# A decoder layer on one core: first key and value weights in four 512-column pieces, factors sent through memory, keys' root from a square root

## The chip, the cores and the metric

The kernel runs on one core of one Trainium2 chip. Times are device microseconds (us) of one launch. Engines are called as in the profile: PE (matrix products), PEld (its weight loads), DVE (vector), ACT (scalar, with tables of functions), POOL (general), SP (here only a queue that issues transfers, DMAs).

## What is computed

One layer of a decoder on 512 tokens of width 1024 in float32. The change touches only the start: the norm of the input, and the key and value columns of the input projection.

```python
def rms_norm(x, g):
    y = xf * lax.rsqrt(jnp.mean(xf * xf, axis=-1, keepdims=True) + EPS)
    return y * g
...
    u = rms_norm(x, norm_mix_g[l])
    proj = u @ w_in[l]
    q = proj[..., :Q_END]                  # 1024 columns, 16 heads of 64
    k = proj[..., Q_END:K_END]             # 256 columns, 4 heads
    v = proj[..., K_END:V_END]             # 256 columns
    glu_in = proj[..., V_END:GLU_END]      # 2048 columns
    gate_attn, gate_conv = jnp.split(proj[..., GLU_END:], 2, axis=-1)
    k = rms_norm(k, k_norm_g[l])
    attn = sliding_window_attention(q, k, v, attn_sinks[l], rel_bias) @ w_attn_o[l]
    conv = conformer_conv(glu_in, ...)
    x = x + (sigmoid(gate_attn) * attn + sigmoid(gate_conv) * conv) @ w_out[l]
    x = x + square(relu(rms_norm(x, norm_mlp_g[l]) @ w_ff1[l])) @ w_ff2[l]
```

## The kernel before

**Numbers in two parts.** Each float32 operand a of a product is split into a high part (a copy rounded to the PE's fast float32 format, made on ACT or DVE) and a low part (a minus the high part, made on DVE or POOL). A product a·b is then three products on PE: high·high, low·high and high·low.

**Input.** The 512 tokens are four tiles of 128. `uTh` and `uTl` hold the high and low part of the normalized input, transposed: 1024 channels in 8 blocks k of 128, by 512 tokens. Tiles 2 and 3 come transposed from memory (`xc`, line 239) and are multiplied by the gain (`act_gain`, `dve_gain`) and then by the token's factor 1/rms. Tiles 0 and 1 come as they are (`load_x`) and are transposed on PE (`x_trans`, line 279). To start early, their first products use the input with the gain alone; the factor, a number for each token, is put in afterwards, when the result leaves PSUM (the argument `scale` of `heads_raw` and `keep_value`). For all later products tiles 0 and 1 are multiplied by their factors too, and split again (`x_scale`, `x_hi`, `x_lo`). `x_scale` needs the factors of a tile in a row, the same row in each of the 128 partitions: `cols_spread` (line 314) makes it with a product on PE into PSUM, `rsb`.

**Keys and values.** The 256 key columns and 256 value columns of the weights come in two halves of 512 rows each (`load_kv`, line 217: four transfers of 512 KB, rows of 256 numbers). High parts lie in `gates`, low parts in `qTt`. For tile 0 the keys and the values are separate products of 256 columns (`first_proj`, line 330: 24 each); for tiles 1 to 3 one product of 512 columns does both (`kv_proj`, line 1376: 24 for each tile). Each tile's result leaves PSUM by three ACT operations and two DVE operations: the raw keys (line 259), their squares (261), the values' high part (345), the squares' sums by head (262) and the values' low part (346).

**Order.** Up to here the order of PE, DVE, ACT and POOL is written out by hand, in the last function (from line 1411): each engine works in the order in which its instructions stand there. The transfers on SP also go in order. After it come all other steps, sorted by positions in units of PE work: first `columns` (the bias table's row `rel`, and two halvings of convolution constants), then the gate and value tiles of the convolution (`ps_g`, `ps_a`: `T_tile`, line 494, 24 products of 512 columns each, which need `uTh` and `uTl` of all four tiles), with `k_norm` (line 390) behind the first of them. `k_norm` makes the 16 factors of the keys on DVE with the integer trick and three Newton steps (`rsqrt`, line 102: 11 small operations behind `mean_eps`), then multiplies the keys. The keys are split (`k_hi`, `k_lo`) and transposed on PE (`k_stage`, `ktp`).

**Warm-up.** `warm_up` (line 206) gives PE products of no use while the first transfers are under way.

Of the kernel before, what the change touches and what calls it, by code (L numbers as in the profile page):

```python
# [8 lines left out]
F32 = mybir.dt.float32  # L9
# [3 lines left out]
ALU = mybir.AluOpType  # L13
# [27 lines left out]
WARM = 6  # L41
FILL = 4
FILL2 = 4
# [11 lines left out]
def tile_hybrid_block(  # L55
# [38 lines left out]
    def bc(ap, n):  # L94
        return ap.partition_broadcast(n)
# [109 lines left out]

    def warm_up(n):
        for _ in range(n):
            pe.matmul(warm, ident, ident, start=True, stop=True)
# [18 lines left out]
    kw_raw = wp.tile([P, KD, 256], F32, name="raw_k", tag="raw", bufs=2)  # L227
    load_kv(kw_raw, Q_END, 0)
    load_kv(kw_raw, Q_END, 1)
    xt.append(load_x(1))  # L230
    vw_raw = wp.tile([P, KD, 256], F32, name="raw_v", tag="raw", bufs=2)
    load_kv(vw_raw, K_END, 0)
    load_kv(vw_raw, K_END, 1)
# [21 lines left out]
    kw, vw = ([w[:, i] for w in (gates, qTt)] for i in range(2))  # L255
# [61 lines left out]

    def x_scale(t, half):
        u = us[t, half] = ps1.tile([P, 4, P], F32, name=f"uc_{t}{half}", tag="tr")
        ve.tensor_tensor(out=u, in0=xc[t][:, both(half), :],  # L320
                         in1=rsb[t].unsqueeze(1).to_broadcast([P, 4, P]), op=ALU.mult)

    def w_hi(w, raw, j, copy):
        copy(w[0][:, 4 * j:4 * j + 4, :], raw[:, 4 * j:4 * j + 4, :])

    def w_lo(w, raw, j, eng):
        ks = slice(4 * j, 4 * j + 4)
        eng.tensor_tensor(out=w[1][:, ks, :], in0=raw[:, ks, :], in1=w[0][:, ks, :].bitcast(F32), op=ALU.subtract)

    def first_proj(w, name):  # L330

        ps = ps1.tile([P, 256], F32, name=f"ps_{name}_0", tag="mm")
        for j in range(2):
            for u in (uTh, uTl):
                for k in range(4 * j, 4 * j + 4):
                    pe.matmul(ps, u[:, k, 0:P], w[0][:, k, :], start=(k == 0 and u is uTh), stop=False)
            yield
        for j in range(2):
            for k in range(4 * j, 4 * j + 4):
                pe.matmul(ps, uTh[:, k, 0:P], w[1][:, k, :], start=False, stop=(k == KD - 1))  # L340
            yield ps
# [23 lines left out]

    def columns():
        rel_ps = ps1.tile([P, P], F32, name="rel_ps", tag="s")
        pe.matmul(rel_ps[0:NQ, :], rb, oh, start=True, stop=True)
        ve.memset(rel, NEG)
        ve.tensor_scalar(out=wcol[:, :, 0:CW], in0=wcol[:, :, 0:CW], scalar1=0.5, scalar2=None, op0=ALU.mult)  # L370
        ve.tensor_scalar(out=lnh, in0=wcol[:, :, CW + 1:CW + 3], scalar1=0.5, scalar2=None, op0=ALU.mult)
        ve.tensor_copy(rel[:, P:2 * P], rel_ps[0:NQ, :])
        nc.sync.dma_start(rel_d, rel)
# [15 lines left out]

    def k_norm():  # L390
        ve.scalar_tensor_tensor(out=gk, in0=gk, scalar=HD ** -0.5, in1=gq, op0=ALU.mult, op1=ALU.mult)
        ve.tensor_scalar(out=nsink, in0=nsink, scalar1=-1.0, scalar2=None, op0=ALU.mult)
        rk = rsqrt(mean_eps(ssk, HD, 16, "k"), 16, "k")
        ve.tensor_tensor(out=k3, in0=k3, in1=rep(rk, HD), op=ALU.mult)
        ve.tensor_tensor(out=k3, in0=k3, in1=gk.unsqueeze(1).to_broadcast([P, 16, HD]), op=ALU.mult)
# [980 lines left out]
    def kv_proj(t, scale=1.0):  # L1376

        ps = ps1.tile([P, S], F32, name=f"ps_kv_{t}", tag="mm")
        for j in range(2):
            for k in range(4 * j, 4 * j + 4):  # L1380
                pe.matmul(ps, uTh[:, k, t * P:(t + 1) * P], gates[:, :, k, :], start=(k == 0), stop=False)
            yield
        for j in range(2):
            for k in range(4 * j, 4 * j + 4):
                pe.matmul(ps, uTl[:, k, t * P:(t + 1) * P], gates[:, :, k, :], start=False, stop=False)
            yield
        for j in range(2):
            for k in range(4 * j, 4 * j + 4):
                pe.matmul(ps, uTh[:, k, t * P:(t + 1) * P], qTt[:, :, k, :], start=False, stop=(k == KD - 1))
            yield  # L1390
        ksum = heads_raw(ps[:, 0:256], kraw, ssk, t, scale)
        vlow = keep_value(t, ps[:, 256:S], scale)
        yield
        ksum()
        vlow()
        yield
# [14 lines left out]
    with tc.manual_schedule(engines=START_ENGINES):  # L1411
        se.activation(roots[:, 0:1], epsc, AF.Sqrt)
        x_square(0, ss0)
        x_trans(0)
        load(0)
# [4 lines left out]
        w_hi(kw, kw_raw, 0, ve.tensor_copy)  # L1420
        w_hi(kw, kw_raw, 1, se.copy)
        r0 = root_steps(root[0], ss0, 1, "x0")
        next(r0)
        for half in range(2):
            x_lo(0, half)
            next(r0)
        w_lo(kw, kw_raw, 0, ve)
        next(r0)
        w_lo(kw, kw_raw, 1, ve)
        kp = first_proj(kw, "k")  # L1430
        next(kp)
        next(kp)
        x_trans(1)
        x_square(1, ss1)
        next(kp)
        ps = next(kp)
        w_hi(vw, vw_raw, 0, se.copy)
        w_hi(vw, vw_raw, 1, se.copy)
        ksum = heads_raw(ps, kraw, ssk, 0, root[0])
# [3 lines left out]
        vp = first_proj(vw, "v")  # L1443
        next(vp)
        next(vp)
        w_lo(vw, vw_raw, 0, ve)
# [35 lines left out]
        vlow()  # L1482
        next(kv)
        for half in range(2):
            x_lo(2, half)
        next(kv)
        kv = kv_proj(2)
        next(kv)
        next(kv)
# [5 lines left out]
        for _ in range(3):  # L1495
            next(kv)
        cols_spread(0, root[0])
# [5 lines left out]
        next(kv)  # L1503
        next(kv)
        next(kv)
        split_hi(0)
        split_lo(0)
        kv = kv_proj(3)
        next(kv)
        next(kv)  # L1510
        cols_spread(1, root[1])
# [5 lines left out]
        for _ in range(4):  # L1517
            next(kv)
        split_hi(1)
        split_lo(1)  # L1520
        split_hi(2)
        split_lo(2)
        next(kv)
        next(kv)
# [47 lines left out]
```

## Time and profile before

| what | value |
|---|---|
| time, median of 3 runs | 753.98 us (753.32 to 754.54) |
| the profiled execution's own time | 753.16 us |
| its span, first to last instruction | 751.4 us |
| PE busy | 744.0 us (99%) |
| DVE, ACT, POOL busy | 616.5, 445.4, 270.8 us |
| first product of the first gate tile `ps_g` | at 33.42 us |
| last product ends | by 747.9 us |

The span is what the profile shows of one execution; 1.76 us of that execution's time lie outside it. A row of the timeline has the start and the length of an instruction or of some merged ones (us), the engine, the line, the operation, the tiles (out<-in), the shapes, and in brackets the idle time ahead of it with what ended it. Merged instructions on an engine overlap a little, so the pace is read from start to start.

### The profile page before, as it was taken

The page shows a single profiled execution, that of the slowest core. Times are in us where ns is not written, and L with a number is a line of the kernel's source. Part 1 is how long each engine was busy: PE and PEld are TensorE (multiplying, and loading weights), DVE is VectorE, ACT ScalarE, POOL GpSimd, SP SyncE. Part 2 cuts the span into 40 slices and gives each one's busy share as a digit, 9 for nine tenths or more (in the row PEclk, how much of TensorE's full clock was granted, in tenths as well). Part 3 has the DMA queues.
Part 4 walks back from the last instruction along what each step waited for, and adds up shares of the span by engine and source line. Part 5 has one row for each costly group of instructions (what it writes and reads, how often), then busy time and mean ns, then how long its engine had stood idle before and what let it go on. Part 6 is the DMA issues. An engine that isn't in the chain of part 4 may idle for free.

```text
span 751.4 us, 11472 instructions
## 1 busy us (share of the span) xinstructions
PE 744.0 (99%) x4358; PEld 653.8 (87%) x4358; DVE 616.5 (82%) x942; ACT 445.4 (59%) x708; POOL 270.8 (36%) x213
## 2 busy tenths in 40 slices
PE   8999999999999999999999999999999999999997
PEld 7889988898888888888888899988998899889986
DVE  6879998888978988887437679899779977998795
ACT  7745467767666566248325457764676467546761
POOL 0364788948675565524450002210121012101210
PEclk9999999999999999999999999999999999999999
DMA  9341041214132122523228206983598359834772
GB/s 334 126 142 57 30 140 57 87 55 139 59 113 85 57 73 96 185 96 105 96 80 307 85 29 114 262 199 98 152 222 199 100 141 221 200 113 127 164 158 112
DMA packets 66071, 97.99 MB, mean 130 GB/s; under 512 B 3248, under 2 KB 36576, under 8 KB 66016
## 3 DMA queue, kind: packets, MB, share of 16 engines
q1 hardware_dynamic: 56768, 79.44, 31.7%
q0 software_dynamic: 9248, 17.83, 13.5%
q8 instruction: 34, 0.56, 0.3%
q14 instruction: 21, 0.17, 0.1%
HBM read 95.13 MB, written 2.12 MB: 129 GB/s over the span
## 4 chain that ended last, share of the span: by engine, by line
PE 98%; DMA 1%; SPq 0%; ACT 0%; DVE 0%; issue 0%; DVEq 0%
PE ps_x L1186 12%; PE ps_z L1191 12%; PE ps_y L1191 6%; PE ps_y L1186 6%; PE ps_z L1186 3%; PE ps_x L1191 3%; PE ps_g L503 2%; PE ps_q L192 2%; PE ps_q L194 2%; PE ps_q L193 2%; PE ps_a L503 2%; PE ps_ta L503 2%; PE ps_a L505 2%; PE ps_g L505 2%; PE ps_ta L505 2%; PE ps_g L504 2%
## 5 line engine op out<-in xcount | busy, mean ns | idle before, releaser
L1157 DVE TENSOR_TENSOR piecel<-block,pieceh 128x1024 fp32r<-128x1024 f32 x112 | 135.9, 1222 | 28.1 <-ACT pieceh L1154 27.8
L1154 ACT CAST pieceh<-block 128x1024 fp32r<-128x1024 f32 x112 | 116.7, 1050 | 69.6 <-DVE block L1147 23.4
L812 DVE SCALAR_TENSOR_TENSOR cv<-h,wcol,cv 128x512 f32<-128x512 f32 x208 | 146.1, 746 | 0.5
L1133 POOL DMA_DIRECT2D block<-in_w_ff_dram x34 | 41.3, 1246 | 287.3 <-DVE piecel L1157 150.3
L1186 PE MATMUL ps_x<-xSh,pieceh 128*128 128x256 f32 x192 | 53.0, 276 | 0.0
L1186 PE MATMUL ps_x<-xSl,pieceh 128*128 128x256 f32 x192 | 53.0, 276 | 0.0
L1186 PE MATMUL ps_x<-xSh,piecel 128*128 128x256 f32 x192 | 53.0, 276 | 0.0
L720 ACT ACTIVATE s<-s,negm 128x257 f32<-128x257 f32 (+1 forms) x64 | 30.4, 479 | 16.4 <-DVE negm L712 16.4
L1191 PE MATMUL ps_z<-piecel,aSh 128*128 128x512 f32 (+1 forms) x98 | 37.9, 387 | 0.0
L1191 PE MATMUL ps_z<-pieceh,aSh 128*128 128x512 f32 (+1 forms) x98 | 37.7, 385 | 0.0
L1191 PE MATMUL ps_z<-pieceh,aSl 128*128 128x512 f32 (+1 forms) x98 | 37.7, 385 | 0.0
L1147 DVE TENSOR_TENSOR block<-block,block 128x1024 f32<-128x1024 f32 x30 | 36.6, 1223 | 0.8 <-DMA block<-in_w_ff_dram 0.3
L804 POOL TENSOR_TENSOR side<-side,tap 128x512 f32<-128x512 f32 x24 | 31.1, 1296 | 15.1 <-ACT tap L803 15.1
L192 PE MATMUL ps_q<-wh_q,uTh 128*128 128x256 f32 x128 | 36.5, 286 | 0.0
L194 PE MATMUL ps_q<-wh_q,uTl 128*128 128x256 f32 x128 | 36.2, 283 | 0.0
L193 PE MATMUL ps_q<-wl_q,uTh 128*128 128x256 f32 x128 | 36.2, 283 | 0.0
L1186 PEld LDWEIGHTS ps_x<-xSh,pieceh 128*128 128x128 f32 x192 | 36.0, 188 | 0.0
L1186 PEld LDWEIGHTS ps_x<-xSl,pieceh 128*128 128x128 f32 x192 | 36.0, 188 | 0.0
L1186 PEld LDWEIGHTS ps_x<-xSh,piecel 128*128 128x128 f32 x192 | 36.0, 188 | 0.0
L744 DVE TENSOR_TENSOR pTl<-ptp,pTh 128x512 fp32r<-128x512 f32 x28 | 19.1, 687 | 17.2 <-ACT pTh L740 17.2
L729 POOL TENSOR_TENSOR s<-s,r 128x1024 f32<-128x1024 f32 (+1 forms) x16 | 26.9, 1684 | 17.0 <-DVE r L724 17.0
L471 POOL TENSOR_TENSOR wl_g<-raw_g,wh_g 128x1024 fp32r<-128x1024 f32 x8 | 19.5, 2432 | 31.8 <-ACT wh_g L467 31.8
(346 smaller groups left out, 2505.0 us busy)
## 6 DMA issues: line engine op xcount, KB each, us to landing
block<-in_w_ff_dram SPq DMA_DIRECT2D x64, 512.0 KB, 5.6
block<-in_w_ff_dram POOLq DMA_DIRECT2D x34, 512.0 KB, 6.9
x<-in_x_dram SPq DMA_DIRECT2D x8, 512.0 KB, 5.0
raw_g<-in_w_in_dram SPq DMA_DIRECT2D x8, 512.0 KB, 5.0
raw_q<-in_w_in_dram SPq DMA_DIRECT2D x8, 512.0 KB, 3.9
raw_a<-in_w_in_dram SPq DMA_DIRECT2D x8, 512.0 KB, 4.3
raw_ta<-in_w_in_dram SPq DMA_DIRECT2D x8, 512.0 KB, 3.9
raw_tc<-in_w_in_dram SPq DMA_DIRECT2D x8, 512.0 KB, 3.9
```

The lines of the kernel that those rows point to most:

```text
L192: pe.matmul(ps, ah, wh, start=first, stop=False)
L193: pe.matmul(ps, ah, wl, start=False, stop=False)
L194: pe.matmul(ps, al, wh, start=False, stop=last)
L503: pe.matmul(ps, wh[:, k, :], ah(k), start=(k == 0), stop=False)
L505: pe.matmul(ps, wl[:, k, :], ah(k), start=False, stop=(k == KD - 1))
L812: ve.scalar_tensor_tensor(out=cps[ct], in0=src, scalar=w, in1=cps[ct], op0=ALU.mult, op1=ALU.add)
L1133: ge.dma_start(tl["raw"][buf][:, ks, :], block(ph, i, j)[:, ks, :], accum_op=ALU.add)
L1147: ve.tensor_tensor(out=o, in0=a, in1=b, op=ALU.add)
L1154: se.copy(piece("h", n), tl["raw"][buf][:, 2 * h:2 * h + 2, :])
L1157: ve.tensor_tensor(out=piece("l", n), in0=tl["raw"][buf][:, 2 * h:2 * h + 2, :], in1=piece("h", n).bitcast(F32), op=ALU.subtract)
L1186: pe.matmul(o, b[:, c, w], a[:, k, :], start=(first and c + q + i == 0), stop=(k == 3 and i == 2), skip_group_check=True)
L1191: pe.matmul(acc[:, cols], a[:, k, w], b[:, c, cols], start=(first and c + i == 0), stop=(k == 3 and i == 2), skip_group_check=True)
```

## The change

1. The key and value weights come in four pieces of 256 rows by all 512 columns (`load_kv(i)`: 512 KB each, rows of 512 numbers), the first ahead of tile 1 of the input and the other three behind it. High and low parts are made by piece.
2. The products of tile 0 are now 24 of 512 columns. `kv_part` gives products by piece and kind ("h": high·high, "l": input's low part, "w": weights' low part), and those of tiles 0 and 1 are interleaved by hand so that they follow the pieces. Tile 1 is transposed ahead of the first product.
3. The factors of tiles 0 and 1 in a row no longer come from `cols_spread`. `spread_first` writes the two columns to memory and reads them back into every partition; `rows_up` copies that to PSUM on ACT.
4. The keys' factors start from a square root on ACT (`k_root`), a reciprocal and one Newton step (`rsqrt_root`): 4 small DVE operations behind `mean_eps` in place of 11.
5. On DVE the two halvings (`channel_halves`), the products of constants (`head_scales`) and the filling of `rel` stand earlier; `split_hi/lo` of the first three weight pieces of the later tiles stand earlier on ACT and POOL. The small loads of `vecs` and `bucket` stand ahead of the first `load`.
6. 8 instead of 6 warm-up products, on a constant 1.0 that is there before `ident`.

The code, cut to its core:

```diff
-WARM = 6
+WARM = 8
+    one = nc.const_aps.tensor(1.0, (P, P), F32)
-            pe.matmul(warm, ident, ident, start=True, stop=True)
+            pe.matmul(warm, one, one, start=True, stop=True)
-    def load_kv(raw, c0, kh):
-        nc.sync.dma_start(raw[:, 4 * kh:4 * kh + 4, :],
-                          w_in[512 * kh:512 * kh + 512, c0:c0 + 256].rearrange("(k p) c -> p k c", p=P))
+    def load_kv(i):
+        nc.sync.dma_start(kv_raw[i // 2][:, 2 * (i % 2):2 * (i % 2) + 2, :],
+                          w_in[256 * i:256 * i + 256, Q_END:Q_END + S].rearrange("(k p) c -> p k c", p=P))
...
+    def spread_first():
+        nc.sync.dma_start(first_d.rearrange("t p -> p t"), roots[:, 0:2])
+        nc.sync.dma_start(first_rows, bass.AP(tensor=first_d.tensor, offset=first_d.offset, ap=[[0, P], [P, 2], [1, P]]))
+    def rows_up():
+        rows = ps1.tile([P, 2, P], F32, name="rows", tag="s")
+        se.copy(rows, first_rows)
+        for t in range(2):
+            rsb[t] = rows[:, t, :]
...
+    def k_root():
+        k2["root"] = sm.tile([P, 16], F32, name="y_k", tag="y16")
+        se.activation(k2["root"], ssk, AF.Sqrt, scale=1.0 / HD, bias=epsc)
     def k_norm():
-        rk = rsqrt(mean_eps(ssk, HD, 16, "k"), 16, "k")
+        rk = rsqrt_root(k2["root"], mean_eps(ssk, HD, 16, "k"), 16, "k")
...
+    def kv_part(t, parts, kinds):
+        if t not in kvs:
+            kvs[t], done[t] = (ps1.tile([P, S], F32, name=f"ps_kv_{t}", tag="mm") if t else aux.tile([P, S], F32, name="ps_kv_0", tag="aux")), 0
+        for i in parts:
+            for kind in kinds:
+                for k in (2 * i, 2 * i + 1):
+                    u, w = {"h": (uTh, gates), "l": (uTl, gates), "w": (uTh, qTt)}[kind]
+                    done[t] += 1
+                    pe.matmul(kvs[t], u[:, k, t * P:(t + 1) * P], w[:, :, k, :], start=done[t] == 1, stop=done[t] == 3 * KD)
...
+        kv_part(0, [0], "hl")
+        w_lo(0, ve)
...
+        kv_part(0, [0], "w")
+        kv_part(0, [1], "hl")
...
+        spread_first()
         load(1)
...
-        cols_spread(0, root[0])
+        rows_up()
+        split_hi(1)
+        split_lo(1)
```

**PE, from the first transposes to the interleaved products.** `tp_u` are the transposed tiles 0 and 1, `ps_k` and `ps_v` tile 0's keys and values, `ps_kv` the joint results (after the change 191 is tile 0, 216 tile 1). Before:

```order
L284 MATMUL tp_u_1_152<-ident,x_102 128x128 x4
L208 MATMUL warm<-ident 128x128 x4
L336 MATMUL ps_k_181<-gates,uTh 128x256 x4
L336 MATMUL ps_k_181<-gates,uTl 128x256 x4
L336 MATMUL ps_k_181<-gates,uTh 128x256 x4
L336 MATMUL ps_k_181<-gates,uTl 128x256 x4
L284 MATMUL tp_u_0_198<-ident,x_108 128x128 x4
L284 MATMUL tp_u_1_203<-ident,x_108 128x128 x4
L340 MATMUL ps_k_181<-qTt,uTh 128x256 x8
```

After:

```order
L283 MATMUL tp_u_1_156<-ident,x_106 128x128 x4
L209 MATMUL warm<-const-float32-1.0 128x128 x4
L283 MATMUL tp_u_0_181<-ident,x_110 128x128 x4
L283 MATMUL tp_u_1_186<-ident,x_110 128x128 x4
L1399 MATMUL ps_kv_191<-gates,uTh 128x512 x2
L1399 MATMUL ps_kv_191<-gates,uTl 128x512 x2
L1399 MATMUL ps_kv_191<-qTt,uTh 128x512 x2
L1399 MATMUL ps_kv_191<-gates,uTh 128x512 x2
L1399 MATMUL ps_kv_191<-gates,uTl 128x512 x2
L1399 MATMUL ps_kv_216<-gates,uTh 128x512 x4
L1399 MATMUL ps_kv_191<-qTt,uTh 128x512 x2
```

The eight transposes of tile 1 moved from behind 16 products of tile 0 to ahead of all of them.

**DVE, the last steps ahead of the first gate tile.** `uc` is the scaled input of a tile in PSUM, `rsb` and `rows` the rows of factors, `vecs` the constants of the heads. Before:

```order
L310 TENSOR_TENSOR uTl<-uc_368,uTh 128x4x128
L262 TENSOR_REDUCE ssk<-sq 128x4
L346 SCALAR_TENSOR_TENSOR vv<-ps_kv_334,vv 128x4x64
L320 TENSOR_TENSOR uc_398<-xc_121,rsb_396 128x512
L320 TENSOR_TENSOR uc_401<-xc_121,rsb_396 128x512
L310 TENSOR_TENSOR uTl<-uc_398,uTh 128x4x128
```

After:

```order
L309 TENSOR_TENSOR uTl<-uc_363,uTh 128x4x128
L376 SCALAR_TENSOR_TENSOR vecs<-vecs 128x64
L377 TENSOR_SCALAR vecs<-vecs 128x16
L261 TENSOR_REDUCE ssk<-sq 128x4
L351 SCALAR_TENSOR_TENSOR vv<-ps_kv_311,vv 128x4x64
L333 TENSOR_TENSOR uc_389<-xc_123,rows 128x512
L333 TENSOR_TENSOR uc_392<-xc_123,rows 128x512
L309 TENSOR_TENSOR uTl<-uc_389,uTh 128x4x128
```

`head_scales` (376 and 377) came in ahead of the last tile's scaling, and the row of factors is now `rows`.

**SP, the transfers behind the input.** `raw_g` and `raw_a` are the weights of the first gate and value tiles. Before:

```order
L239 DMA xc_119<-in_x_cols_dram 128x1024
L454 DMA raw_g_157<-in_w_in_dram 128x4x256 x2
L1456 DMA vecs<-in_vectors_dram 128x144
L1457 DMA bucket<-in_buckets_dram 32x144
L454 DMA raw_q_0_453<-in_w_in_dram 128x4x256
L454 DMA raw_a_255<-in_w_in_dram 128x4x256 x2
```

After:

```order
L239 DMA xc_121<-in_x_cols_dram 128x1024
L1424 DMA vecs<-in_vectors_dram 128x144
L1425 DMA bucket<-in_buckets_dram 32x144
L466 DMA raw_g_163<-in_w_in_dram 128x4x256 x2
L322 DMA first_d<-roots 128x2x1
L466 DMA raw_a_260<-in_w_in_dram 128x4x256 x2
L323 DMA first_rows<-first_d 128x256
L466 DMA raw_q_0_436<-in_w_in_dram 128x4x256
```

The two transfers of the factors are new; between them stand the two of `raw_a`.

More of the change, by code (lines that the diff above doesn't have):

```diff
@@ L321, in x_scale, with kv_piece, kv_raw_piece, w_hi @@
                          in1=rsb[t].unsqueeze(1).to_broadcast([P, 4, P]), op=ALU.mult)
[L323 to L341, printed above, removed]
+    def kv_piece(w, i):
+        return w[:, :, 2 * i:2 * i + 2, :].rearrange("p i k c -> p k i c")
+    def kv_raw_piece(i):
+        return kv_raw[i // 2][:, 2 * (i % 2):2 * (i % 2) + 2, :].rearrange("p k (i c) -> p k i c", i=2)
+    def w_hi(i, copy):
+        copy(kv_piece(gates, i), kv_raw_piece(i))
+    def w_lo(i, eng):
+        eng.tensor_tensor(out=kv_piece(qTt, i), in0=kv_raw_piece(i), in1=kv_piece(gates, i).bitcast(F32), op=ALU.subtract)
     def keep_value(t, ps, scale=1.0):
@@ L1373, in tile_hybrid_block, with kv_keep @@
                            "S4": e[3] + 16, "P3": e[3] + 17})
[L1376 to L1396, printed above, removed]
+    kvs, done = {}, {}
+    def kv_part(t, parts, kinds):
[7 more added lines that the diff above has]
+                    pe.matmul(kvs[t], u[:, k, t * P:(t + 1) * P], w[:, :, k, :], start=done[t] == 1, stop=done[t] == 3 * KD)
+    def kv_keep(t, scale=1.0):
+        ksum = heads_raw(kvs[t][:, 0:256], kraw, ssk, t, scale)
+        vlow = keep_value(t, kvs[t][:, 256:S], scale)
+        return ksum, vlow
     def root_steps(y, ss, w, tag):
@@ L1414, in tile_hybrid_block @@
         x_trans(0)
+        nc.sync.dma_start(vecs[:, 0:2 * HD + NQ], bc(vectors[0], P))
+        nc.sync.dma_start(bucket, buckets)
         load(0)
@@ L1419, in tile_hybrid_block @@
             x_hi(0, half)
-        w_hi(kw, kw_raw, 0, ve.tensor_copy)
-        w_hi(kw, kw_raw, 1, se.copy)
+        w_hi(0, ve.tensor_copy)
         r0 = root_steps(root[0], ss0, 1, "x0")
         next(r0)
[L1424 to L1427, printed above, removed]
+        x_lo(0, 0)
         next(r0)
[L1429 to L1432, printed above, removed]
         x_trans(1)
+        kv_part(0, [0], "hl")
+        w_lo(0, ve)
+        next(r0)
         x_square(1, ss1)
[L1435 to L1439, printed above, removed]
+        w_hi(1, se.copy)
         for half in range(2):
@@ L1502, in tile_hybrid_block @@
             x_lo(0, half)
[L1503 to L1511, printed above, removed]
+        kv_part(3, range(4), "h")
+        ksum, vlow = kv_keep(2)
+        head_scales()
+        ksum()
+        vlow()
+        split_hi(2)
+        split_lo(2)
         for half in range(2):
@@ L1516, in tile_hybrid_block @@
             x_lo(1, half)
[L1517 to L1524, printed above, removed]
+        ve.memset(rel, NEG)
+        kv_part(3, range(4), "lw")
+        ksum, vlow = kv_keep(3)
+        ksum()
+        vlow()
+        k_root()
         for _, _, fn, args in sorted(events, key=lambda e: e[:2]):
```

84 lines of the change are left out of this document (44 added, 40 removed).

## Prediction

> **What bounds the kernel now.** I read the page first, then the busy time by stretch, then PE's timeline. The page's span and its chain of waits:
>
> ```profile
> span 751.4 us, 11472 instructions
> PE 98%; DMA 1%; SPq 0%; ACT 0%; DVE 0%; issue 0%; DVEq 0%
> ```
>
> The chain that ends last is PE. Busy time by stretch (stretch, its length, PE busy with the count of instructions, clock, DMA share, GB/s):
>
> ```profile
> 0.00:33.42 33.42, 30.18 (x167) 1.00 0.72 259
> 33.42:747.90 714.48, 713.87 (x4193) 1.00 0.44 125
> ```
>
> From 33.42, where the first gate tile starts, PE is busy for 713.87 of 714.48 us. Nothing behind it can be hidden or gained, as long as the other engines keep up. The change rewrites what lies before. So the question is one number: when does the first product of `ps_g` start? PE's timeline has it, and what leads there:
>
> ```profile
> 1.47 2.93 PE L208 MATMUL warm<-ident 128*128 128x128 f32 x12 [1.47 <-POOL eps_ln L117]
> ...
> 5.17 1.06 PE L208 MATMUL warm<-ident 128*128 128x128 f32 x8
> 7.69 0.71 PE L336 MATMUL ps_k<-gates,uTh 128*128 128x256 f32 x4 [1.47 <-DVE roots L1402]
> ...
> 9.35 0.74 PE L336 MATMUL ps_k<-gates,uTh 128*128 128x256 f32 x4 [0.28 <-ACT gates L324]
> ...
> 10.40 1.03 PE L284 MATMUL tp_u<-ident,x 128*128 128x128 f32 x8
> ...
> 18.82 0.61 PE L316 MATMUL rsb<-ident,roots 128*128 128x128 f32 x4
> 19.18 0.72 PE L340 MATMUL ps_v<-qTt,uTh 128*128 128x256 f32 x4
> ...
> 21.59 1.99 PE L1381 MATMUL ps_kv<-gates,uTh 128*128 128x512 f32 x8
> 23.41 1.98 PE L1385 MATMUL ps_kv<-gates,uTl 128*128 128x512 f32 x8
> ...
> 31.18 1.98 PE L1389 MATMUL ps_kv<-qTt,uTh 128*128 128x512 f32 x8
> 33.10 0.39 PE L368 MATMUL rel_ps<-bucket 32*16 32x128 f32 x2
> 33.42 0.50 PE L503 MATMUL ps_g<-uTh,wh_g 128*128 128x512 f32 x1
> ```
>
> Useful products start at 7.69 and then run almost without a gap. Eight products of 512 columns take 1.82 us in the stream (21.59 to 23.41), 0.2275 each; 1.92 where the kind of product changes behind them (31.18 to 33.10), so a change costs 0.1. Two `rsb` products take 0.36 (18.82 to 19.18), `rel_ps` 0.32 (33.10 to 33.42). The early starts hang on data; ACT's and DVE's waits for the weights and for tile 1:
>
> ```profile
> 8.24 1.05 ACT L324 CAST gates<-raw_k 128x1024 fp32r<-128x1024 f32 x1 [1.37 <-DMA raw_k<-in_w_in_dram]
> 9.49 1.06 ACT L276 ACTIVATE kraw<-x 128x1024 f32<-128x1024 f32 x1 [0.19 <-DMA x<-in_x_dram]
> ...
> 10.87 1.04 ACT L324 CAST gates<-raw_v 128x1024 fp32r<-128x1024 f32 x1
> ```
>
> ```profile
> 6.85 0.69 DVE L324 CAST gates<-raw_k 128x1024 fp32r<-128x1024 f32 x1 [0.63 <-DMA raw_k<-in_w_in_dram]
> ```
>
> The 512 KB transfers land one behind the other: first weight piece 6.85, second 8.24, tile 1 at 9.49, so 1.39 for a piece in rows of 256 numbers and 1.25 for a tile.
>
> **Part by part: the start.** Now a single weight piece stands ahead of tile 1, which so lands at 6.85 + 1.25 = 8.10 if pieces land as before. How much rows of 512 numbers bring, no row shows for this place. The nearest rows are the transfer rates around the first pieces (length, clock, DMA share, GB/s):
>
> ```profile
> 3.40:6.80 3.40, 1.00 0.89 287
> 6.80:12.20 5.40, 1.00 1.05 397
> ```
>
> At the second stretch's rate the first 3.40 us would take 2.46: a gain of up to 0.94; the other end is none. A loss is out, since there are half as many rows to fetch. The share was already 0.89, so little time was empty, and I take a quarter, 0.25: tile 1 lands at 7.85 (7.16 to 8.10).
>
> PE must transpose tile 1 before its first useful product. Eight transposes last from 10.40 to 11.19 before (the next product starts there), 0.79, so the first product is at 7.85 + 0.05 + 0.79 = 8.69, a microsecond later than now. That is the cost of the reorder. In return the stream behind it is shorter:
>
> - 96 products of 512 columns at 0.229 (just above the stream's 0.2275): 21.98. Before, tile 0 took 48 products of 256 columns.
> - One pair `rsb` 0.36; three changes of kind 0.30; `rel_ps` 0.32.
> - One wait of 0.15, at the second piece's products: ACT squares tile 1 first (9.49 to 10.87 before, 1.38) and then makes the piece's high part (1.05), so it is ready 2.5 behind tile 1's landing; PE is there after 0.84 + 6 x 0.229 + 0.1 = 2.3.
>
> Sum 23.11: `ps_g` starts at 8.69 + 23.11 = 31.80, against 33.42: 1.62 gained. The pieces behind tile 1, 1.3 apart, land at 9.2, 10.5 and 11.8; PE needs the third's high part near 12.7 and the fourth's near 17: hidden, but the third by less than a microsecond once ACT has made it (1.05), and PE waits as long as it is later than that.
>
> **Part by part: DVE's chain to the same point.** The second product of `ps_g` reads `uTl` of the last scaled tile, tile 1. The rows of this chain, DVE's first, then ACT's and POOL's:
>
> ```profile
> 8.93 1.22 DVE L328 TENSOR_TENSOR qTt<-raw_k,gates 128x1024 fp32r<-128x1024 f32 x1
> ...
> 19.60 1.29 DVE L320 TENSOR_TENSOR uc<-xc,rsb 128x512 f32<-128x512 f32 x2
> ...
> 21.19 1.28 DVE L310 TENSOR_TENSOR uTl<-uc,uTh 128x512 fp32r<-128x512 f32 x2
> 22.66 0.42 DVE L262 TENSOR_REDUCE ssk<-sq 128x4 f32<-128x256 f32 x1 [0.18 <-ACT sq L261]
> 23.02 0.48 DVE L346 SCALAR_TENSOR_TENSOR vv<-ps_kv,roots,vv 128x256 fp32r<-128x256 f32 x1
> ...
> 35.37 2.41 DVE L371 TENSOR_SCALAR eps_ln<-wcol 128x16 f32<-128x16 f32 x1
> ...
> 41.81 3.30 DVE L395 TENSOR_TENSOR kraw<-kraw,vecs 128x1024 f32<-128x1024 f32 x1
> ```
>
> ```profile
> 13.89 1.14 ACT L306 CAST uTh<-xc 128x512 fp32r<-128x512 f32 x2
> ...
> 21.78 0.48 ACT L259 ACTIVATE kraw<-ps_kv,roots 128x256 f32<-128x256 f32 x1 [0.27 <-PE ps_kv L1389]
> ...
> 22.51 0.47 ACT L345 ACTIVATE vv<-ps_kv,roots 128x256 fp32r<-128x256 f32 x1
> ```
>
> ```profile
> 35.06 2.63 POOL L471 TENSOR_TENSOR wl_g<-raw_g,wh_g 128x1024 fp32r<-128x1024 f32 x1
> ...
> 40.80 3.23 POOL L471 TENSOR_TENSOR wl_a<-raw_a,wh_a 128x1024 fp32r<-128x1024 f32 x1 [3.05 <-ACT wh_a L467]
> ```
>
> Forty products, one wait and a change after 8.69, at about 18.1, PE makes `rsb`; tile 2 is scaled from 18.8 (its neighbour's gain, 1.14, ends then). From there to `uTl` of tile 1's first half: three tiles at 2.4 (two scalings 1.2, two low parts 1.2) and 1.25 of the last one, 8.45; three kept results at 0.75 (0.35 and 0.4), 2.25; about 0.6 for ACT, which puts 1.2 us for each kept result and 1.14 for each `x_hi` in one queue; 0.8 for some ten hand-overs between engines, an estimate; `head_scales` 0.2. That is 12.3, and 0.65 on top for POOL. The rows: L371 took 2.41 us for 16 numbers while POOL worked at `wl_g` to 37.69, and L395 3.30 against 1.22 for the same shape (L328) while POOL worked to 44.03; both ended just after POOL. `head_scales` reads SBUF only, as these do, and falls into POOL's `wl_a`: ACT makes `wh_a` behind `rows_up`, 25.5 to 26.5, POOL works some 2.5 from there, DVE comes at 28.35 (two tiles and a half of the four behind it) and goes on at 29.0. Chain's end 18.8 + 12.3 + 0.65 = 31.75, 32.5 if the hand-overs double; PE's second product is at 31.80 + 0.33 = 32.1. It is covered, barely. The Trainium skill's page "SBUF — State Buffer" (section "SBUF: two separate sides") calls the port pair shared by DVE and POOL an exclusive lock that the loser waits out, for DVE operations with two SBUF inputs among others; the two rows agree; without that wait the chain would end 0.65 earlier, the sum would be the same, and the rival on this chain would have less than half its chance.
>
> **The row of factors.** Waits are added on SP, ACT and DVE. SP holds `first_rows` until `first_d` has landed, with the q weights queued behind (used far later); ACT's `rows_up` waits for it with `wh_a`, `x_hi` of tile 0 and the kept tile 2 behind; DVE's scaling of tile 0 waits for that at about 25.9. Transfers alone or nearly alone, with their KB and microseconds to landing:
>
> ```profile
> raw_q<-in_w_in_dram SPq DMA_DIRECT2D x1, 512.0 KB, 3.3
> ```
>
> ```profile
> rel_d<-rel SPq DMA_DIRECT2D x1, 24.0 KB, 4.4
> ```
>
> ```profile
> bias<-rel_d SPq DMA_DIRECT2D x1, 512.0 KB, 4.4
> ```
>
> `first_d` goes out behind `raw_g`. Nine transfers of 512 KB at 1.3 and small ones of 0.5 lie between tile 1's landing and `raw_g`'s: 7.85 + 12.2 = 20. At best `first_d` lands half a microsecond behind, 20.6, and `first_rows` 3.3 later, 23.9; at worst each takes 4.4 from 20, 28.8. I take 25, since the queue is nearly empty by then and little is moved; it is needed at 25.3 on ACT. No cost, with no slack to speak of.
>
> **The keys.** The shorter root takes 7 small operations off DVE; `k_root` adds a wait on ACT for the last sum, with the table load and the first gate's evaluation behind it, which wait for `ps_g` 5 us later anyway. PE waits for the keys once:
>
> ```profile
> 46.92 0.39 PE L505 MATMUL ps_g<-uTh,wl_g 128*128 128x512 f32 x1
> 47.25 0.53 PE L409 MATMUL ktp_h<-ident_r,k2h 128*128 128x128 f32 x4
> ```
>
> ```profile
> 45.20 2.00 ACT L401 CAST k2h<-kraw 128x1024 fp32r<-128x1024 f32 x2 [4.48 <-DVE kraw L395]
> ```
>
> The row at 46.92 should be followed after 0.23 and is followed after 0.33: 0.10, and it goes, since the keys no longer wait for POOL's 3.23 and the root is shorter. Everything else there was hidden.
>
> **Sum.** 1.62 + 0.10 = 1.72. Against the profiled execution's own 753.16 (span 751.4, 1.76 outside) that is 751.44. The median of the runs shown is 0.82 above this execution, so for a median I say 753.98 - 1.72 = 752.3. Within 0.2% (1.5 us) a measurement of this kernel can hardly tell a change; the forecast stands at that edge.
>
> **Rivals.** *Late factors (slower).* Mechanism: the write and read of memory take longer than PE's own spread. From the landing R it is 6.45 to `uTl` of tile 1 (25.3 to 31.75, with POOL's part), so `ps_g`'s second product waits once R passes 25.65. The gain is gone at R = 27.4, the point from which the kernel is slower than before, and R = 28.8 gives 1.4 on top, 755.4. For it: two landings of 4.4 in rows. Against: `raw_q`'s 3.3 for 512 KB, and `first_rows` moves a quarter of that. Chance 0.11, of which 0.03 slower by over 0.2%.
>
> *The clock falls.* The rows show two paces: the warm-up products start 0.23 apart from 1.47, 0.11 apart from 5.17. PE stands idle now from 6.2 to 7.69; after the change from 6.2 to 7.9. If that brings the slow pace back for the length it had, 2.9 us, half of this is lost, 1.45: gain 0.3, 753.7. The clock column of the two stretches says 1.00, slow pace or not, so it can't be seen there; but after 1.47 us of idle time the eight transposes at 10.40 started 0.11 apart, the fast pace. Chance 0.05. The Trainium skill ("TensorE: Matmul & The Clock Gate", section "HAM oscillation — how this bites in real kernels") states that an idle gap over some 3.4 us halves the clock; 1.7 is below it, and no run here shows such a gap.
>
> *DVE's chain ends last.* One more microsecond in its hand-overs and waits for ACT, and it ends at 32.75 instead of 31.75: 0.65 of the gain is lost, 752.95. For it: the margin of 0.35. Against: before, tile 1's keys waited on PE (`kraw` at 21.78), not on DVE. Chance 0.10.
>
> *Data earlier.* The first piece lands 0.7 earlier still: gain 2.4, 751.6. For it: the 287 GB/s. Against: DVE and ACT, not sped up, have little slack. Chance 0.13.
>
> *The gain is given back* at a place that no row shows: 754. Chance 0.03.
>
> **How the numbers follow.** My forecast, a gain of 1.2 to 2.1, has 0.58. Its time is 752.3. About six tenths of it (0.36) lies above 1.5; with 0.13 from early data, faster is 0.49. Slower is 0.03, and the rest, 0.48, is within 0.2%. The range, from early data with 0.6 of spread between runs (751.0) to the gain gone (753.9), leaves out the slow end and some of either side.
>
> **What would show it.** Right: tile 1's squares start near 7.9, the first `ps_kv` near 8.7, `ps_g` near 31.8, no wait at `ktp`, ACT's `rows` without a DMA wait. Wrong: PE idle between 9 and 31 beyond 0.5 us; `rows` waiting past 25.5; `ps_g` after 32.6 or before 31.

## The result, and the profile after

| | before | after |
|---|---|---|
| time, median | 753.99 us (753.32 to 754.54) | 759.30 us (758.19 to 760.08) |
| time of the profiled execution, and its span | 753.16, 751.4 | 758.19, 756.4 |
| tile 1 of the input lands | 9.47 | 8.72 |
| row of factors lands | (none) | 30.99 |
| first product of `ps_g` | 33.42 | 36.90 |
| first product of `ps_a`, 24 products later | 38.99 | 44.24 |

The ratio is 1.0070 (95% interval 1.0057 to 1.0082): slower by 0.7%, where 752.3 us and faster was forecast. Times of landing, here and below, are issue plus time to landing from the trace's DMA records. The page of after, span and chain of waits:

```profile
span 756.4 us, 11420 instructions
PE 95%; DMA 3%; DVE 1%; ACT 0%; issue 0%; SPq 0%; DVEq 0%
```

The chain was 98% PE and is 95% now, with 3% of DMA. PE's waits in the first 60 us (total, times, longest) name the place:

```profile
PE ps_g L515 <- ACT uTh L305: 4.2, 1, 4.2
```

PE's timeline of after around the start and around the first gate tile:

```profile
4.33 1.91 PE L283 MATMUL tp_u<-ident,x 128*128 128x128 f32 x8
...
8.86 1.06 PE L283 MATMUL tp_u<-ident,x 128*128 128x128 f32 x8 [1.66 <-DMA x<-in_x_dram]
9.68 0.71 PE L1399 MATMUL ps_kv<-gates,uTh 128*128 128x512 f32 x2
...
32.34 0.39 PE L381 MATMUL rel_ps<-bucket 32*16 32x128 f32 x2
...
36.90 0.77 PE L515 MATMUL ps_g<-uTh,wh_g 128*128 128x512 f32 x1 [4.17 <-ACT uTh L305]
37.62 0.80 PE L516 MATMUL ps_g<-uTl,wh_g 128*128 128x512 f32 x1
...
38.64 0.63 PE L515 MATMUL ps_g<-uTh,wh_g 128*128 128x512 f32 x1
...
40.83 0.39 PE L515 MATMUL ps_g<-uTh,wh_g 128*128 128x512 f32 x1
...
44.24 0.39 PE L515 MATMUL ps_a<-uTh,wh_a 128*128 128x512 f32 x1
```

The products of keys and values end at 32.34 and `rel_ps` takes 0.32, so `ps_g` could have started at 32.66, 0.76 ahead of before. It starts at 36.90, 3.48 behind before. And its first products are slow: 24 take 7.34 us (36.90 to 44.24) instead of 5.57 (33.42 to 38.99), 1.77 more. The busy time by stretch of after (stretch, length, PE, clock, DMA share, GB/s) shows why:

```profile
36.90:44.24 7.34, 7.34 (x25) 0.77 0.52 172
36.90:752.90 716.00, 715.44 (x4192) 1.00 0.44 124
```

The granted clock was 0.77 in that stretch: PE came out of the wait at half pace. In windows of 0.05 us the clock is 0.50 from about 36.96 to 40.37, for 3.41 us, and 1.00 on both sides. 3.48 and 1.77 are 5.25 us, and the span grew by 5.0. What PE waited for is in the chain of after, in order of time (start, length, what):

```profile
15.90 10.58 DMA first_d<-roots
26.50 4.49 DMA first_rows<-first_d
...
34.09 0.80 DVE vecs L376
...
35.62 0.61 DVE uc L333
36.26 0.59 ACT uTh L305
36.90 0.77 PE ps_g L515
```

The row of factors: 1 KB written by `first_d` took 10.58 us from its issue, the read of it 4.49. ACT stood for it with everything behind it in its queue, then DVE for ACT:

```profile
8.74 1.07 ACT L275 ACTIVATE kraw<-x 128x1024 f32<-128x1024 f32 x1 [1.12 <-DMA x<-in_x_dram]
...
31.01 0.38 ACT L327 COPY rows<-first_rows 128x256 f32<-128x256 f32 x1 [5.00 <-DMA first_rows<-first_d]
```

```profile
7.51 0.69 DVE L343 CAST gates<-raw_kv 128x1024 fp32r<-128x1024 f32 x1 [0.55 <-DMA raw_kv<-in_w_in_dram]
...
31.42 1.29 DVE L333 TENSOR_TENSOR uc<-xc,rows 128x512 f32<-128x512 f32 x2 [4.68 <-ACT rows L327]
34.09 0.80 DVE L376 SCALAR_TENSOR_TENSOR vecs<-vecs 128x64 f32<-128x64 f32 x1
```

While `first_d` was on its way the transfer engines were busy and moved little (windows of after: stretch, length, PE, clock, DMA share, GB/s):

```profile
22.40:26.50 4.10, 4.10 (x20) 1.00 0.83 67
```

### The profile page after: what moved, and what is told of

Its sections match the earlier page's. It is cut to its first block, busy times and chain, and to the rows that moved or that the text cites. A ratio compares the mean times of both kernels' runs of the same rounds, so it can differ in the third digit from the quotient of the medians.

```text
span 756.4 us, 11420 instructions
## 1 busy us (share of the span) xinstructions
PE 745.7 (99%) x4334; PEld 654.6 (87%) x4334; DVE 611.7 (81%) x935; ACT 445.5 (59%) x710; POOL 269.8 (36%) x213
## 4 chain that ended last, share of the span: by engine, by line
PE 95%; DMA 3%; DVE 1%; ACT 0%; issue 0%; SPq 0%; DVEq 0%
PE ps_x L1198 12%; PE ps_z L1203 12%; PE ps_y L1203 6%; PE ps_y L1198 6%; PE ps_z L1198 3%; PE ps_x L1203 3%; PE ps_g L515 2%; PE ps_q L191 2%; PE ps_g L516 2%; PE ps_q L193 2%; PE ps_q L192 2%; PE ps_a L515 2%; PE ps_g L517 2%; PE ps_ta L515 2%; PE ps_a L517 2%; PE ps_ta L517 2%
## 5 line engine op out<-in xcount | busy, mean ns | idle before, releaser
L1169 DVE TENSOR_TENSOR piecel<-block,pieceh 128x1024 fp32r<-128x1024 f32 x112 | 135.9, 1222 | 28.8 <-ACT pieceh L1166 28.6
L515 PE MATMUL ps_g<-uTh,wh_g 128*128 128x512 f32 x64 | 26.9, 420 | 4.2 <-ACT uTh L305 4.2
```

What stands on the lines that cost most here:

```text
L515: pe.matmul(ps, wh[:, k, :], ah(k), start=(k == 0), stop=False)
L1169: ve.tensor_tensor(out=piece("l", n), in0=tl["raw"][buf][:, 2 * h:2 * h + 2, :], in1=piece("h", n).bitcast(F32), op=ALU.subtract)
```

## The experiments

Theory A: the four-byte writes of `first_d` are slow and hold up every transfer queued near them; PE waits for what comes of it and runs at half pace behind the wait. Rival B: any way through memory and back is too late here. Rival C: the new start in four pieces lost the time. "Spread" below is PE's own way of making a row of factors, `cols_spread`, as before.

**PE's own spread again.** The changed kernel without the way through memory.

```diff
-        spread_first()
-        rows_up()
+        cols_spread(0, root[0])
         kv_part(3, range(4), "h")
+        cols_spread(1, root[1])
```

> All of the change but the factors of tiles 0 and 1, which PE spreads again with two products as before. Theory A (the four-byte writes hold the transfers up, PE then waits 4.2 us for the factors and runs at half clock behind that): ps_g starts near 32.9 (32.66 without a wait in the trace of after, and 0.3 for the two products), no slow products behind it, 753.4 us (752.8 to 754.0). Theory B (any round trip through memory is too late here, whatever its element size): the same. Theory C (the start in four pieces lost the time, the factors only lie beside it): 757 or more.

Measured: 753.39 us, ratio to before 0.9992 (0.9983 to 1.0001). No wait at `ps_g`:

```profile
33.25 0.50 PE L515 MATMUL ps_g<-uTh,wh_g 128*128 128x512 f32 x1
...
38.82 0.39 PE L515 MATMUL ps_a<-uTh,wh_a 128*128 128x512 f32 x1
```

Its busy time in the stretch in which after moved 67 GB/s at a share of 0.83:

```profile
22.40:26.50 4.10, 4.10 (x21) 1.00 0.46 160
```

`raw_a`, the second gate's weights, lands at 23.14 and 24.49; in after, 28.05 and 30.11. Its DMA issues here, then in after (KB, median us to landing):

```profile
raw_a<-in_w_in_dram SPq DMA_DIRECT2D x2, 512.0 KB, 6.6
```

```profile
raw_a<-in_w_in_dram SPq DMA_DIRECT2D x2, 512.0 KB, 11.8
```

All of the loss lies in the way through memory; C is out.

**The wait filled.** Sixteen products of no use behind `rel_ps`.

```diff
+        idle = aux.tile([P, S], F32, name="idle", tag="aux")
+        for _ in range(16):
+            pe.matmul(idle[:, 0:P], one, one, start=True, stop=True)
```

> The change as it is, with 16 products of no use on constants put behind rel_ps, to keep PE busy through most of its wait for the factors. If the slow products behind the wait (24 of ps_g in 7.3 us where 5.5 is usual) come from PE having been idle: ps_g starts at 36.9 as before, its 24 products take 5.5, and the time falls by 1.8, to 757.5. If they are slow because their data comes late or for another reason: no change, 759.3.

Measured: 757.88 us, 1.0045 (1.0031 to 1.0059): by medians 3.6 us slower than the kernel before beside it (754.27), where after was 5.3 slower than its own (753.99), so 1.7 less. The row of factors is as late (`ps_g` at 37.09), but PE idles only 0.5 ahead of it, and the stretch to `ps_a` shows the full clock:

```profile
37.09:43.15 6.06, 5.83 (x25) 1.00 0.56 177
```

6.06 instead of 7.34 for the same 24 products. None of its four executions has a mean clock under 0.998; five of the six of after have 0.994 or 0.995. The half pace comes from PE's idle time; the wait itself stays.

**The same way through memory, in rows of 512 bytes.** PE turns the two columns into two rows first; the write then has 2 elements of 512 bytes instead of 256 of four.

```diff
-        nc.sync.dma_start(first_d.rearrange("t p -> p t"), roots[:, 0:2])
+        nc.sync.dma_start(first_d, xt[0][0:2, 0:P])
...
+        rt = ps1.tile([2, P], F32, name="rt", tag="s")
+        pe.matmul(rt, roots[:, 0:2], ident, start=True, stop=True)
+        ve.tensor_copy(xt[0][0:2, 0:P], rt)
```

> The factors still go through memory, but PE first turns the two columns into two rows, so that the write is two elements of 512 bytes and not 256 of four. Theory A: first_d lands within 1 us of raw_g's second piece (22.4), first_rows 3.5 to 4.5 behind, 26 to 27.5, raw_a before 26; ps_g starts at 32.7 to 33.4 and the time is 753.2 to 754.3. Theory B: first_d lands near 25 or later, first_rows near 29 or later, 757 or more.

Measured: 753.10 us, 0.9988 (0.9979 to 0.9997). `first_rows`, which waits for the write, could be issued at 21.60, 0.1 us ahead of the landing of the second `raw_g` (21.70): the write held nothing up. SP's timeline, then ACT's:

```profile
17.69 0.30 SPq L322 DMA_DIRECT2D first_d<-x  x1
18.09 0.92 SPq L466 DMA_DIRECT2D raw_a<-in_w_in_dram  x2
21.60 0.34 SPq L323 DMA_DIRECT2D first_rows<-first_d  x1
```

```profile
27.14 0.38 ACT L327 COPY rows<-first_rows 128x256 f32<-128x256 f32 x1 [0.54 <-DMA first_rows<-first_d]
```

The read, now beside `raw_a`, took 5.5, and ACT waited half a microsecond. `raw_a` landed at 25.49 and 26.81, 2.3 later than with PE's spread and the second piece later than expected; nothing waited on PE for it. B falls: the way through memory is fast enough, if it is not made of four-byte neighbours.

**The write kept, but unused.** PE's own spread, with `spread_first()`, the write and the read back, still issued at its place. Against after:

```diff
-        rows_up()
+        cols_spread(0, root[0])
...
+        cols_spread(1, root[1])
```

> PE spreads the factors as in the run with that change alone, but the four-byte write and the read back are still issued, and nothing on PE, DVE or ACT uses what they bring until the bias table is filled. Theory A: first_d still takes some 10 us and raw_a's two pieces land near 28 and 30, while without these transfers they land before 25; the time is within 0.5 of the kernel without them. Theory C: the time stays at 757 or more. If raw_a lands as late without the transfers, they do not hold their neighbours up.

Measured: 757.45 us, 1.0041 (1.0026 to 1.0055). A miss, and the most telling one. Nobody uses the row, and most of the loss is there. In the trace, which is of the slowest of its six executions (755.58 to 759.62), `raw_a`, behind the write in the queue, lands at 31.44 and 32.62, and ACT, which makes its high part, holds `x_hi` of tile 0 behind it (ACT's timeline, then PE's wait):

```profile
32.70 1.05 ACT L479 CAST wh_a<-raw_a 128x1024 fp32r<-128x1024 f32 x1 [4.30 <-DMA raw_a<-in_w_in_dram]
```

```profile
PE ps_g L515 <- ACT uTh L305: 2.7, 1, 2.7
```

So the write costs twice over: through the row itself, and through its neighbours. The waits of the two paths overlap in after.

**Half of the elements.** PE's own spread; one tile's column alone is written, unused and not read back.

```diff
-        nc.sync.dma_start(first_d.rearrange("t p -> p t"), roots[:, 0:2])
-        nc.sync.dma_start(first_rows, bass.AP(...))
+        nc.sync.dma_start(first_d[0:1].rearrange("t p -> p t"), roots[:, 0:1])
```

> PE's own spread, and the four-byte write of one tile's column alone, 128 elements, unused and not read back. If the price goes by the number of elements (11.0 us from issue to landing for 256), this one lands 5 to 6 us behind its issue, the first weights of the second gate land 2 to 3 us late instead of 7, and the time is near 753.4 or up to 1 us above it. If the price is a fixed one of such a write (a wait for what is queued ahead, or for the memory), it lands 9 to 11 us behind its issue, and the weights come as late as with 256, 755.5 to 757.5.

Measured: 756.99 us, 1.0033 (1.0019 to 1.0046). 128 elements take as long as 256, and the loss is there without the read back:

```profile
first_d<-roots SPq DMA_DIRECT2D x1, 0.5 KB, 12.0
```

It lands at 27.13, 5.83 behind the second `raw_g` (21.30); the 256 took 5.92 in the experiment above and 4.09 in after. The price isn't in proportion to the number of elements.

**The elements apart, by 512 bytes and by 64.** PE's own spread; all 256 elements are written again, unused and not read back, into a larger tensor.

```diff
-    first_d = dr.tile([2, P], F32, name="first_d")
+    first_d = dr.tile([2, P, P], F32, name="first_d")
-        nc.sync.dma_start(first_d.rearrange("t p -> p t"), roots[:, 0:2])
+        nc.sync.dma_start(first_d[:, :, 0].rearrange("t p -> p t"), roots[:, 0:2])
```

By 64 bytes: `dr.tile([2, P, 16], ...)`.

> PE's own spread, and the four-byte write of all 256 elements, each 512 bytes from the next in memory, unused and not read back. If 11.0 us come from many writers into the same few lines of memory, the write now lands within 5 us and the second gate's weights land where they do without it (23.1 and 24.5), time near 753.4. If each element costs by itself (about 0.04 us), it lands about 11 us behind its issue as before, the weights are 4 to 8 us late, and the time is 755.5 to 757.5.

> PE's own spread, and the four-byte write of all 256 elements, each 64 bytes from the next, unused and not read back; eight of them fall into 512 bytes. If what costs is writers in the same 64 bytes or less, it lands as with 512 bytes between, 0.2 us behind the transfer ahead of it, the second gate's weights are at 23.0 and 24.4, and the time is 753.6. If it is writers in the same 512 bytes, and the price goes by how many share them (4 to 6 us behind the transfer ahead for 128), 8 of them take about 0.3 us, with the weights 0.3 late and the same time. If the price goes by 512 bytes shared at all, or by the whole stretch of memory being small, it lands 4 us or more behind, and the time is 755.5 to 757.5.

Measured: 753.59 us, 0.9989 (0.9980 to 0.9998), and 753.39, 0.9994 (0.9985 to 1.0003). The DMA issues of the two (KB, us to landing; in each the time is spent behind `raw_g` in the queue), and the stretch of the first:

```profile
first_d<-roots SPq DMA_DIRECT2D x1, 1.0 KB, 6.2
```

```profile
first_d<-roots SPq DMA_DIRECT2D x1, 1.0 KB, 6.9
```

```profile
22.40:26.50 4.10, 4.10 (x21) 1.00 0.49 173
```

256 four-byte writes now land about 0.2 us behind the second `raw_g`, and `raw_a` is where it is without them (23.01 and 24.36; 23.12 and 24.45). The same elements, as small and as many: what costs is that they are packed together in memory. Packed, the 256 share 1 KB; 64 bytes apart they lie in 16 KB. No run tells apart whether it is the step to the next element that counts, under 64 bytes, or that so many writes fall into one small stretch. The Trainium skill's page "DMA: Bandwidth & Descriptors" (section "Specifications") says that transfers below 512 bytes are read, changed and written back; that alone would have made these two slow as well, and they are not.

**The keys' root as before.** PE's own spread, and `rsqrt` on DVE.

```diff
-        rk = rsqrt_root(k2["root"], mean_eps(ssk, HD, 16, "k"), 16, "k")
+        rk = rsqrt(mean_eps(ssk, HD, 16, "k"), 16, "k")
...
-        k_root()
```

> The kernel with PE's own spread (753.4), and the keys' root made by DVE alone as before, with its 7 small operations more and no root on ACT. If the keys' wait of 0.10 us on PE before came from DVE's slow multiplication beside POOL (3.30 us for one), which the moved scaling of the heads has taken away, the root is hidden: the products in front of the keys' transposes stay 0.23 apart and the time is within 0.3 of 753.4. If the shorter root was needed, the transposes wait on PE, by about 0.1 us if the order of the work alone counts, up to 0.7 (7 small operations at about 0.1 each), and the time is 753.5 to 754.1.

Measured: 753.05 us, 0.9989 (0.9980 to 0.9997), and no wait at the keys (PE, then DVE):

```profile
47.06 0.40 PE L517 MATMUL ps_g<-uTh,wl_g 128*128 128x512 f32 x1
47.30 0.46 PE L421 MATMUL ktp_h<-ident_r,k2h 128*128 128x128 f32 x4
```

```profile
38.65 1.23 DVE L407 TENSOR_TENSOR kraw<-kraw,vecs 128x1024 f32<-128x1024 f32 x1
```

0.24 from start to start, and 0.22 with the new root (46.76 to 46.98). The shorter root is worth nothing. What took the 0.10 away is, by the traces, part 5. Before, the second halving (L371, 2.41 us beside POOL) and the scaling of the heads stood ahead of the keys, and the multiplication of 3.30 began at 41.81, inside POOL's `wl_a` (40.80 to 44.03). With both moved ahead it is done by 39.9, before POOL's next work (40.94), in 1.23. No run puts part 5 back alone.

**The first piece in two transfers.** PE's own spread; the piece loaded in rows of 256 numbers, as before.

```diff
-    load_kv(0)
+    for c in (0, 256):
+        nc.sync.dma_start(kv_raw[0][:, 0:2, c:c + 256],
+                          w_in[0:256, Q_END + c:Q_END + c + 256].rearrange("(k p) c -> p k c", p=P))
```

> PE's own spread, and the first weight piece loaded in two transfers with rows of 256 numbers, as the rows were before, instead of one transfer with rows of 512. If the longer rows are why that piece lands at 7.49 instead of 6.83, it now lands at about 6.9, tile 1 at 8.2, the first product with the weights starts near 9.1 instead of 9.74, and the time is 752.8. If the place or the start of the queue is the reason, the piece lands at 7.5 or later (up to 0.5 for the added transfer), and the time is 753.4 to 753.9.

Measured: 753.09 us, 0.9989 (0.9979 to 0.9998). The piece landed at 6.97. That looked like the rows; the next two runs show that one execution can't tell.

**One more execution of each kernel**, unchanged.

> The kernel before, unchanged, looked at once more: where do its first weight piece and tile 1 land? In the trace shown of it they landed at 6.83 and 9.47; in nine executions of the changed start the first piece, one transfer at the same place in the queue, landed anywhere from 6.49 to 8.42, half of them at 7.5 or later. If the landing varies from execution to execution whatever the rows are, it need not be 6.83 here: anything from 6.5 to 8.4, with tile 1 2.64 behind it and the first gate tile 23.95 behind tile 1, so up to 35.0. If the new rows make it late, it is again within 0.1 of 6.83, and the first gate tile starts within 0.1 of 33.42. Time 754 to 755 either way.

> The changed kernel, unchanged, looked at once more: is the late row of factors the same in another execution? By the theory of the four-byte write it lands 4 to 6 us behind the second piece of the first gate's weights (4.1 in the trace shown), the row of factors 4.5 behind that, PE waits 4 to 6 us for the first gate tile and then runs at half pace for some 3.3 us; time 758 to 760.5. If the trace shown was an odd execution, the wait is under 3 us and the time under 758.

Measured, one time each: 754.62 and 758.09 us. In this execution of before the first piece landed at 7.63 and tile 1 at 10.40 (6.83 and 9.47 in the trace shown), and `ps_g` started at 34.40. In the changed start the piece landed, by execution, at 6.49, 7.16, 7.49, 7.49, 7.50, 7.56, 7.62, 7.84, 7.93 and 8.42. With the new rows the landing varies by 1.9 us; with rows of 256 numbers four executions have 6.83, 6.97, about 7.2 and 7.63, inside that range. That the rows shift it by a few tenths is neither shown nor excluded. The trace of before that the forecast rests on was an early one.

In after, `first_d` landed 3.9 behind `raw_g` and the row 4.2 later, close to what was expected (4 to 6, and 4.5), but the wait was 2.0 and not 4 to 6, a miss: PE was itself late, since tile 1 landed 0.5 later than in the trace shown and its transposes and the first products ran at half pace, which cost 1.3. Its timeline, and its windows:

```profile
9.32 1.94 PE L283 MATMUL tp_u<-ident,x 128*128 128x128 f32 x8 [2.37 <-DMA x<-in_x_dram]
...
36.55 0.80 PE L515 MATMUL ps_g<-uTh,wh_g 128*128 128x512 f32 x1 [2.03 <-ACT uTh L305]
```

```profile
9.30:11.30 2.00, 1.98 (x9) 0.50 1.05 410
36.55:43.81 7.26, 7.26 (x24) 0.77 0.51 173
```

**Products first.** On the kernel with the first piece in two transfers.

```diff
-        x_trans(1)
         kv_part(0, [0], "hl")
+        x_trans(1)
```

> The kernel with the first piece in two transfers (753.1), and PE takes the four products of tile 0 with the first piece's high part ahead of tile 1's transposes instead of behind them. The first product then starts at about 7.8 instead of 9.45. If the stream is bound by its first product, as the forecast's sum had it, the first gate tile starts 0.5 earlier than 32.95 (four products of 0.23, less 0.4 of waiting for the low part) and the time is 752.6. If it is bound by the second piece (landed 9.78, its high part made by ACT at 10.94, waited for on PE), the waiting moves there, the first gate tile starts within 0.2 of 32.95, later if anything, since tile 1's transposes come later, and the time is 753.0 to 753.5.

Measured: 752.70 us, 0.9983 (0.9974 to 0.9992), the fastest of all and ahead of both kernels; its interval overlaps that of the kernel without the swap (0.9979 to 0.9998), so the swap isn't shown to help. PE's timeline, of one of its slower executions (753.67), shows no gain from it:

```profile
8.13 0.70 PE L1401 MATMUL ps_kv<-gates,uTh 128*128 128x512 f32 x2 [1.67 <-DVE roots L1413]
...
11.59 0.74 PE L1401 MATMUL ps_kv<-gates,uTh 128*128 128x512 f32 x2 [0.76 <-ACT gates L345]
...
33.59 0.50 PE L517 MATMUL ps_g<-uTh,wh_g 128*128 128x512 f32 x1
```

The first product starts early, PE waits for the second piece instead, and `ps_g` starts 24.49 behind tile 1's landing (9.10), as it does without the swap (24.45). Why the median is 0.4 lower stays open.

## Why the prediction was wrong, point by point

**The stream: right.** From tile 1's landing to `ps_g` the forecast has 31.80 - 7.85 = 23.95 us. After: 32.66 - 8.72 = 23.94, had nothing held `ps_g`. The agreement to 0.01 is luck: the first product came 0.96 behind the landing, not 0.84, and the rest took 22.98, not 23.11, since the wait of 0.15 for the second piece isn't among PE's waits. With PE's own spread, about 0.5 more: 24.46, 24.46, 24.43, 24.45, 24.45, 24.49 and 24.48 in seven executions of kernels whose `ps_g` waits for nothing (the one with rows of 512 bytes among them, whose added PE products cost the same). Before: 23.95 and 24.00. So the reorder shortens nothing behind tile 1; it gains what tile 1 lands earlier, one piece of 1.3, and the forecast's sum had that.

**Tile 1's landing: 8.72 instead of 7.85.** The forecast took the first piece 0.25 earlier and called a loss out of the question ("A loss is out"). The runs show a spread of 1.9 us between executions, in which one trace of before is one draw. In the likeliest case (7.5 for the piece) the gain is there all the same: before would then have tile 1 near 10.1. With the row through PE the median is 753.39 against 754.27, 0.9 us less, where the forecast's sum less 0.5 for the spreads is 1.2. The interval of that run just reaches 1 (1.0001); four other kernels whose `ps_g` waits for nothing have ratios of 0.9988 and 0.9989 with intervals just below 1, a fifth 0.9994 (0.9985 to 1.0003), so the start gains about 0.1%, hardly clear of noise.

**The row of factors: the step that failed.** "I take 25" and "No cost, with no slack to speak of". It landed at 30.99, 6.0 later, in three parts: tile 1 landed 0.87 later; from there to the second `raw_g` it took 13.68 instead of 12.2, since `vecs` and `bucket`, "small ones of 0.5", took 1.85 (17.94 to 19.79; from 0.4 to 1.8 in the other executions of the changed start); and write and read took 4.09 and 4.49 behind that, where 25 allows 5 for both. The upper bound, two landings of 4.4, held for the pair, but hung from 20 instead of 22.4; and with the unused writes the pair took 5.92 and 5.2, beyond it. It was written down, with its mechanism, as the rival *Late factors* at 0.11 and 755.4. No row of before showed a write of four-byte neighbours; the row nearest to it, `rel_d` with 4.4, was the safe one to take, and the forecast took a value nearer the good end than the bad one (23.9 to 28.8), "since the queue is nearly empty by then and little is moved". In the trace little was moved indeed, 67 GB/s, but at a DMA share of 0.83.

**What hangs on the row: right, but only half of it.** From the landing R to the second product of `ps_g` the forecast has 6.45. After: 37.62 - 30.99 = 6.63; with rows of 512 bytes 33.81 - 27.12 = 6.69. L376 was held up by POOL's `wl_a` as foreseen:

```profile
32.45 2.35 POOL L483 TENSOR_TENSOR wl_a<-raw_a,wh_a 128x1024 fp32r<-128x1024 f32 x1 [5.35 <-ACT wh_a L479]
```

POOL ends at 34.80 and L376, from 34.09, at 34.89. One reading behind it was loose: of the two rows that "both ended just after POOL", L371 did, by 0.09, but L395 ended 1.08 behind it (45.11 and 44.03), nearly the 1.22 that the same shape takes alone (L328). Missing was the write's effect on its neighbours: `first_d` was priced as a transfer that only its reader waits for. Unused, write and read back still cost 3.2 us (757.45 against 754.27), and the write of half of the elements alone 2.7 (756.99 against 754.28).

**The clock: the right mechanism at another place.** The forecast had half pace as a rival behind the idle time ahead of tile 1, 1.45 lost, 0.05. That happened in two of the traced executions of the changed start: in after's second one (1.94 instead of 1.06 for the transposes; `ps_g`, without its wait, 25.3 behind tile 1 instead of 23.9) and in the one with the unused writes, just behind the transposes. The sure case is the wait that the forecast didn't expect: 1.77 us in after, on top of the wait. *Late factors* had no such term.

The clocks of the executions without a trace say more, as an estimate. In the traces one stretch of half pace gives a mean clock of 0.998, two give 0.995. Of 64 executions of six kernels whose `ps_g` waits for nothing (all but the one with products first), 12 have 0.998 or less, with times of 754.5 to 755.5; of 72 of before, 7; of 11 with products first, none. So 0.05 was too low for this rival. In after five of six executions have 0.994 or 0.995, the traced one 0.998: a second stretch would be most of the 1.1 us by which the median, 759.30, lies above the traced execution's 758.19.

**The keys: 0.10, right in size,** not from the root, and by the traces from part 5.

**The sum.** Forecast 751.44 for a profiled execution. `ps_g` starts 36.90 - 31.80 = 5.10 later (0.86 of it the start, 4.24 the wait); half pace 1.77; that makes 758.31, and 758.19 was measured. DVE's own chain, data earlier and a loss given back elsewhere were not what decided.

## What to carry to other kernels

Price a transfer by the shape of its elements in memory, not by its bytes: a kilobyte turned from a column into a row by four-byte neighbours cost more than a transfer of 512 KB, and the transfers queued behind it came 5 to 6 us late as well. If a trace has no row for an operation on the chain, forecast with the bad end, and add what a wait does to the clock behind it. And take a start-up time from more than one execution before a term of a few tenths is built on it.

## What the runs showed of the hardware

- 128 or 256 four-byte writes into neighbouring addresses: 3.9 to 5.9 us behind the transfer ahead, 67 GB/s at a DMA share of 0.83 meanwhile. The same 256 writes 64 or 512 bytes apart: about 0.2 us. Two writes of 512 bytes: none. Why neighbours are slow isn't shown, only that they are.
- PE's half pace needs no long idle time, and lasted equally long each time: in all six stretches of it (one in after, two in its second execution, two with the unused writes, one with half of the elements) the clock was 0.50 for 3.4 us, which takes up to 1.7 us. Behind a wait of 1.3 us (half of the elements) the clock was granted at 0.50 for over 3 us, beginning 1.3 us after PE had gone on:

```profile
36.01:39.20 3.19, 3.19 (x9) 0.50 0.88 283
```

  The Trainium skill's page "TensorE: Matmul & The Clock Gate" puts the threshold at an idle gap of some 3.4 us (section "HAM oscillation — how this bites in real kernels") and states windows of that length that run freely (section "What's actually happening"). Waits of 4.2, 2.7, 2.0 and 1.3 us ahead of `ps_g` were all followed by half pace, one of 0.5 was not; and of eleven idle stretches of 1.3 to 3.6 us ahead of tile 1's transposes, two were (2.4 and 3.6), one of 2.4 and one of 2.9 were not. Of the six gaps that half pace followed only two reached 3.4 (4.2 and 3.6), so that threshold doesn't hold here. Windows that run freely could be why of two gaps of 2.4 one was followed by it and one not; that isn't shown, and a wholly idle window of 3.4 us has no room in a gap of 1.3.
